# A recurrent scan by halves of the matrix array, more banks for one attention, and a reciprocal root on GpSimd

## Chip, cores and metric

One core of a Trainium2 chip runs the whole program. The metric is device time in microseconds (us) of one execution, lower is better; each kernel is given by the median of several runs. A profile of one execution lies beside the times. Engines are written as in it: PE (TensorE), DVE (VectorE), ACT (ScalarE), POOL (GpSimd), SP (SyncE, which issues most of the loads).

## What is computed

Two transformer blocks in float32, one after the other, on 256 tokens of width 1024. The first block has two layers; layer 0 works on 512 tokens (256 of context, 256 latent), layer 1 puts out the latent ones. Each layer is a mixer and a gated feed-forward net (width 2816), each between a norm with modulation (shift and scale from a conditioning vector) and a norm with a gate. The mixer of layer 0 is what the change is mostly about: a gated delta rule, run over the tokens forwards and backwards in chunks of 64, beside a latent attention (MLA) of 8 heads. Per chunk the rule computes

```
v_new = u_i - w_i @ s                     # s: state, 64x64 per head
o_i   = qd_i @ s + qk_i @ v_new
s     = s * gl_i + kd_i.T @ v_new
```

and the MLA is `softmax(q @ k.T) @ v` with 256 keys for context queries and 512 for latent ones. The second block (sparse attention, a convolution branch, a feed-forward net of 4096) is not touched.

## The kernel before, in words

Every dense weight is loaded from memory as float32, split into a high part (`whi`, rounded by ACT, L270) and a rest (`wlo`, a subtraction, L272), and each product is three matmuls (`mm3`, L552 to L556). `Weights.turn` (L227) says which engine does the subtraction of each next tile: `W.turn("PPPPPP", "V")` gives six tiles to GpSimd and then all to VectorE; `W.turn("V")` gives all to VectorE. A tile has two halves of 128x512, so two subtractions.

PSUM has eight banks of 128x512. In layer 0's mixer they are three of kind "g", two of "s", and one each of "tp", "po" and "gv"; `acc(K)` takes from "s" and `aux(K)` from "g" (L1881). A buffer tagged with `bufs=n` has n copies in turn.

The scan is `gdn_run` (L1216). For each of four rounds and each direction d, `gdn_operands` (L1140) makes u, w, q and decayed k for one tile of 128 tokens (two chunks), in three "g" banks, with 16 + 16 matmuls of 64x64 (L1158, L1160) and four transposes (L1163); ACT copies the results to SBUF (L1165 to L1169), and a matrix Q comes back from memory by a DMA on SP's queue (L1171). Then `gdn_state` (L1183) runs twice, once per chunk: state product w @ s and qd @ s in one bank (L1192), v_new by VectorE (L1195), the update kd.T @ v_new in a second bank (L1199: four matmuls of 64 rows and 128 columns, of whose result two 64x64 blocks on the diagonal are used), state times decay by GpSimd (L1206), the update added by VectorE (L1207), the output product in a third bank (L1210: eight matmuls, all from one half of the rows to the other half of the partitions), and the outputs written or added by `gdn_o` (L1175). A chunk of the tile is addressed as a = 0 or 1, which is the half of the partitions that it lies on; the forward direction takes a = 0, 1, the backward one 1, 0.

After the scan, in program order, come `gdn_post` (norm and gate), six `mod_chunk` calls (L361, matmuls of modulation weights) and `l0_mla` (L787). The MLA has four pairs of heads. For a pair it makes q and k (bank "s" for pairs 0 and 1, "g" for 2 and 3), then per tile of 128 queries `attend` (L665) makes scores in one bank per head, maximum on VectorE, exponential on ACT, transposes on PE (L681) into the same bank, copies to SBUF, and the product with v (L689) in bank "po". `attend` gets two banks' kinds: ("s", "s") for pairs 0 and 1, ("s", "g") for 2 and 3. Its tiles `p` and `pt` have `K.np` = 2 buffers.

Which instruction stands where in an engine's queue is chosen when the kernel is built (`schedule_with_timeline_sim=True`, L2174): program order gives priority, so instructions of the scan, the modulation and the MLA are interleaved on each engine. On the chip each engine then works its queue in order and waits on semaphores.

At the end of layer 0, `linear_deep` (L618) computes the feed-forward net's last product for four tiles of tokens, tile after tile at the end. `post_norm` (L517) consumes it: ACT sums squares, `rstd2` (L340) and `newton` (L310) take the reciprocal root in 8 instructions on one column (L343, L319, three times L322 and L323), VectorE adds the scaled result to h (L542), ACT sums the squares of h (L514), and `norm_tile` (L503) takes a second root, scales the identity by it (L507) and transposes and scales the tile with it on PE (`to_features`, L489), from where ACT and VectorE modulate and split it (L498, L496, L306, L307). Layer 1 then starts with `linear_tok` on its input weights (L1428). Its first six weight tiles are subtracted on GpSimd.

Of the kernel before, what the change touches and what calls it, by code (L numbers as in the profile page):

```python
# [309 lines left out]
def newton(K, v, post=1.0, tag=""):  # L310


    nc = K.nc
    p, n = v.shape[0], v.shape[-1]
    y = sbt(K, [128, 1 if n == 1 else 64], F32, "rsy%d" % (n == 1) + tag, 4)[:, :n][:p]
    t = sbt(K, [128, 1 if n == 1 else 64], F32, "rst%d" % (n == 1) + tag, 2)[:, :n][:p]
    a = -(float(post) / 8192.0) ** (1.0 / 27.0)
    guess = 1597463007.0 + math.log2(-a) * 2 ** 23 - 2.0 ** 31
    nc.vector.tensor_scalar(y.bitcast(I32), v.bitcast(I32), -0.5, float(round(guess)), op0=ALU.mult, op1=ALU.add)  # L319
    for _ in range(3):  # L320
        if n == 1:
            nc.vector.tensor_scalar(t, y, y, v, op0=ALU.mult, op1=ALU.mult)  # L322
            nc.vector.tensor_scalar(y, t, -3.0 * a * a, y, op0=ALU.add, op1=ALU.mult)  # L323
        else:
            nc.vector.tensor_tensor(t, y, y, op=ALU.mult)
            nc.vector.tensor_tensor(t, t, v, op=ALU.mult)
            nc.vector.scalar_tensor_tensor(y, t, -3.0 * a * a, y, op0=ALU.add, op1=ALU.mult)
        a = -2.0 * a ** 3
    return y
# [10 lines left out]
def rstd2(K, ss, tag=""):  # L340

    v = sbt(K, [128, 1], F32, "rsv1" + tag, 2)
    K.nc.vector.tensor_scalar(v, ss[:, 0:1], ss[:, 1:2], D * EPS, op0=ALU.add, op1=ALU.add)  # L343
    return newton(K, v, math.sqrt(D), tag)
# [158 lines left out]
def norm_tile(K, x, ss, coef, hi, lo, t):  # L503


    dg = cut(K, [128, 128], F32, "ndg", 2)
    K.nc.vector.tensor_scalar_mul(dg, K.ident, rstd2(K, ss, "n"))  # L507
    to_features(K, x, coef, hi, lo, t, dg)
# [8 lines left out]
def post_norm(K, G, hdst, after, sq=True, T=2, row=None, held=True):  # L517
# [6 lines left out]
    def consume(c, t, ps):  # L524
# [9 lines left out]
        if c == 1:  # L534
            r = rstd2(K, ss, "p")
# [251 lines left out]
def l0_mla(K, O):  # L787
# [49 lines left out]
    wq = None  # L837
    for pair in range(4):
# [21 lines left out]
        for t in range(4):  # L860
            n = 256 if t < 2 else 512

            def score(pss):
                tk = slice(t * 128, (t + 1) * 128)
                for hh in range(2):
# [4 lines left out]
                   ("s", "g") if late else ("s", "s"))  # L870
        nc.scalar.copy(O[:, pair, :], rb)
        nc.vector.tensor_tensor(O[:, pair, :], po, O[:, pair, :], op=ALU.mult)

# [309 lines left out]
def gdn_state(K, d, first, t, a, u, wq, kd, Q, S):  # L1183
    nc = K.nc
    r = slice(64 * a, 64 * a + 64)
    o = slice(64 - 64 * a, 128 - 64 * a)
# [9 lines left out]
    pS, po = aux(K), aux(K)  # L1196
    for p in range(4):
        c = slice(p * 128, (p + 1) * 128)
        nc.tensor.matmul(pS[:, c], kd[r, c], vn[r, c], start=True, stop=True)  # L1199
    pSv = pS.rearrange("p (q c) -> p q c", q=4)  # L1200
    for hh in range(2):
        x = slice(hh * 64, hh * 64 + 64)
        if first:
            nc.vector.tensor_copy(S[x, :, x], pSv[x, :, x])
        else:
            nc.gpsimd.tensor_tensor(S[x, :, x], S[x, :, x], bc(K.glc[d][x, t, a, :], [64, 4, 64], 2), op=ALU.mult)  # L1206
            nc.vector.tensor_tensor(S[x, :, x], S[x, :, x], pSv[x, :, x], op=ALU.add)  # L1207
    for h in range(8):
        hs = slice(h * 64, h * 64 + 64)
        nc.tensor.matmul(po[o, hs], Q[r, h, :], vn[r, hs], start=True, stop=True)  # L1210
    if not first:
        gdn_o(K, t, a, o, ps)
    gdn_o(K, t, a, o, po)


def gdn_run(K):  # L1216
    K.owritten = set()
    for i in range(4):
        for d in range(2):
            t = i if d == 0 else (1, 0, 3, 2)[i]  # L1220
            ops = gdn_operands(K, d, t)
            for a in ((0, 1) if d == 0 else (1, 0)):
                gdn_state(K, d, i == 0 and a == d, t, a, *ops, K.S[d])
# [651 lines left out]
def layer0(K):  # L1875
# [18 lines left out]
    with Banks(K, {"acc": 5, "aux": 2, "gv": 1}):  # L1894
# [22 lines left out]
        with Pool(K, "ff"):  # L1917
# [8 lines left out]
            with Pool(K, "ffd"):  # L1926
                G = [gate_row(K, 0, s, 1) for s in range(2)]

                def src(g, nk):
# [5 lines left out]
                                      lambda t, ss, x: norm_tile(K, x, ss, coef_mod(K, 1, 0, st(t)), K.uh, K.ul, t), T=4,  # L1935
                                      held=False))
# [31 lines left out]
def layer1(K, h):  # L1968
# [5 lines left out]
    with Pool(K, "l1o"):  # L1974
        load_const(K, "rest", K.cur)
        oh, ol = cut(K, [128, 8, 256], FR), cut(K, [128, 8, 256], FR)
        W.turn("PPPPPP", "V")
# [200 lines left out]
```

## Time and profile before

| | us |
|---|---|
| median of 3 runs | 2125.01 |
| lowest and highest | 2121.82, 2138.47 |
| the profiled execution | 2124.6 |
| its span, first to last instruction | 2122.8 |

Times within the execution are counted from the first instruction. A timeline row gives start and length in us, engine, line of the code, operation, tile written and tiles read (buffer numbers left out), shapes, and the count of instructions merged in the row; in brackets the idle time of the engine before it and what ended it. A float32 matmul of the code shows as two MATMUL records. The granted clock is TensorE's, 1.00 for 2.4 GHz and 0.50 for 1.2 GHz; a value between is a mean over a stretch.

### The profile page before, as it was taken

What the parts mean: (1) busy time and instruction counts of PE and PEld (TensorE: products, weight loads), DVE (VectorE), ACT (ScalarE), POOL (GpSimd) and SP (SyncE); (2) the same over time, 40 slices, a digit from 0 to 9 for tenths busy, and PEclk for the clock granted to TensorE, in tenths of its full rate; (3) what the DMA queues carried; (4) which work ended last, traced back from release to release, by engine and by line L of the source; (5) the groups of instructions that cost most, each with busy time, mean ns of one, the idle gap of its engine ahead of it and who ended that gap; (6) DMA issues with size and microseconds to landing.
All of it is one profiled execution on the core that took longest, in us unless ns stands there. A gap on an engine that the chain in (4) does not pass through costs nothing.

```text
span 2122.8 us, 31144 instructions
## 1 busy us (share of the span) xinstructions
PE 1991.6 (94%) x11656; PEld 1626.7 (77%) x11656; DVE 1315.5 (62%) x2729; ACT 924.7 (44%) x1620; POOL 242.1 (11%) x312
## 2 busy tenths in 40 slices
PE   6989799889999999979898999998999999989998
PEld 3868468768888778868666888897788789868886
DVE  5557457766777754454786555575765558576644
ACT  4533443354222233343565443564554445555532
POOL 2120212301000000020401001110200021020000
PEclk8999789899999999989898999998999999999999
DMA  8344542132568542213235664522656535055551
GB/s 284 90 120 101 179 130 66 46 109 80 179 213 279 164 158 90 89 53 120 70 99 159 184 194 137 155 87 62 197 179 190 180 97 147 21 169 184 188 188 66
DMA packets 186951, 291.88 MB, mean 137 GB/s; under 512 B 28472, under 2 KB 75704, under 8 KB 186800
## 3 DMA queue, kind: packets, MB, share of 16 engines
q1 hardware_dynamic: 172720, 272.54, 41.2%
q0 software_dynamic: 5472, 16.13, 2.4%
q10 hardware_dynamic: 8608, 1.23, 0.5%
q8 instruction: 91, 1.49, 0.3%
q14 instruction: 60, 0.49, 0.1%
HBM read 281.44 MB, written 8.41 MB: 137 GB/s over the span
## 4 chain that ended last, share of the span: by engine, by line
PE 85%; DVE 5%; DMA 4%; ACT 3%; issue 2%; POOL 1%; SPq 0%; ACTq 0%; DVEq 0%; POOLq 0%
PE acc L554 19%; PE acc L556 19%; PE acc L555 19%; PE s L554 3%; PE s L555 2%; PE s L556 2%; PE po L689 2%; PE tp L890 2%; PE po L1540 1%; PE tp L1540 1%; DMA wraw<-in_w_mod_dram 1%; PE gv L373 1%; PE aux L728 1%; PE aux L489 1%; PE g L1199 1%
## 5 line engine op out<-in xcount | busy, mean ns | idle before, releaser
L272 DVE TENSOR_TENSOR wlo<-wraw,whi 128x512 fp32r<-128x512 f32 (+4 forms) x772 | 483.4, 670 | 299.1 <-ACT whi L270 283.3
L270 ACT CAST whi<-wraw 128x1024 fp32r<-128x1024 f32 (+4 forms) x420 | 413.5, 990 | 496.4 <-PE acc L556 192.9
L554 PE MATMUL acc<-whi,u 128*128 128x512 f32 (+3 forms) x1320 | 508.5, 388 | 15.4 <-ACT u L306 9.6
L556 PE MATMUL acc<-whi,u 128*128 128x512 f32 (+3 forms) x1320 | 505.2, 384 | 1.7 <-DVE u L307 1.7
L555 PE MATMUL acc<-wlo,u 128*128 128x512 f32 (+3 forms) x1320 | 506.0, 385 | 0.2 <-DVE wlo L272 0.2
L554 PEld LDWEIGHTS acc<-whi,u 128*128 128x128 f32 x1320 | 251.3, 191 | 66.0 <-ACT u L306 11.6
L556 PEld LDWEIGHTS acc<-whi,u 128*128 128x128 f32 x1320 | 251.0, 190 | 50.4 <-DVE u L307 3.8
L555 PEld LDWEIGHTS acc<-wlo,u 128*128 128x128 f32 x1320 | 251.4, 191 | 47.4 <-DVE wlo L272 1.4
L554 PE MATMUL acc<-u,whi 128*128 128x512 f32 (+1 forms) x480 | 171.0, 362 | 1.8 <-ACT u L306 1.7
L555 PE MATMUL acc<-u,whi 128*128 128x512 f32 (+1 forms) x480 | 171.0, 358 | 0.2 <-DVE u L307 0.2
L556 PE MATMUL acc<-u,wlo 128*128 128x512 f32 (+1 forms) x480 | 171.1, 360 | 0.0
L272 POOL TENSOR_TENSOR wlo<-wraw,whi 128x512 fp32r<-128x512 f32 (+1 forms) x68 | 84.7, 1276 | 409.7 <-ACT whi L270 409.7
L432 DVE SCALAR_TENSOR_TENSOR msum<-mraw,u,msum 128x512 f32<-128x512 f32 x140 | 100.8, 747 | 15.2 <-DMA mraw<-in_w_mod_dram 14.1
L554 PEld LDWEIGHTS acc<-u,whi 128*128 128x128 f32 x480 | 91.0, 191 | 17.4 <-issue 2.6
L555 PEld LDWEIGHTS acc<-u,whi 128*128 128x128 f32 x480 | 91.9, 192 | 15.0 <-issue 1.7
L556 PEld LDWEIGHTS acc<-u,wlo 128*128 128x128 f32 x480 | 91.5, 191 | 15.0 <-issue 1.7
L307 DVE TENSOR_TENSOR u<-aux,u 128x512 fp32r<-128x512 f32 (+2 forms) x96 | 59.5, 632 | 41.0 <-ACT u L306 40.8
L554 PE MATMUL acc<-whi,dxh 128*128 128x512 f32 x176 | 69.7, 396 | 1.9 <-ACT dxh L306 1.9
L306 ACT CAST u<-aux 128x512 fp32r<-128x512 f32 (+2 forms) x96 | 50.6, 543 | 47.6 <-PE aux L728 34.9
L555 PE MATMUL acc<-wlo,dxh 128*128 128x512 f32 x176 | 69.6, 396 | 0.0
L556 PE MATMUL acc<-whi,dxl 128*128 128x512 f32 x176 | 69.0, 396 | 0.0
L307 DVE TENSOR_TENSOR dxl<-u,dxh 128x1024 fp32r<-128x1024 f32 x22 | 26.7, 1225 | 52.5 <-ACT dxh L306 52.5
(521 smaller groups left out, 3089.6 us busy)
## 6 DMA issues: line engine op xcount, KB each, us to landing
wraw<-in_w_up_dram SPq DMA_DIRECT2D x64, 512.0 KB, 4.0
wraw<-in_w_down_dram SPq DMA_DIRECT2D x64, 512.0 KB, 4.0
mraw<-in_w_mod_dram SPq DMA_DIRECT2D x56, 512.0 KB, 4.7
wraw<-in_w_ffn_down_dram SPq DMA_DIRECT2D x44, 512.0 KB, 3.8
wraw<-in_w_mod_dram SPq DMA_DIRECT2D x40, 512.0 KB, 5.9
wraw<-in_w_ffn_gate_dram SPq DMA_DIRECT2D x48, 256.0 KB, 3.1
wraw<-in_w_ffn_up_dram SPq DMA_DIRECT2D x48, 256.0 KB, 3.6
wraw<-in_w_ffn_gate_dram SPq DMA_DIRECT2D x20, 512.0 KB, 4.5
```

The lines of the kernel that those rows point to most:

```text
L270: self.K.nc.scalar.copy(hi, raw)
L272: e.tensor_tensor(lo[:, k], raw[:, k], hi.bitcast(F32)[:, k], op=ALU.subtract)
L306: (hi_eng or nc.scalar.copy)(hi, src)
L307: nc.vector.tensor_tensor(lo, src, hi.bitcast(F32), op=ALU.subtract)
L373: nc.tensor.matmul(ps[32 * j:32 * j + 32, :], K.cl[:, g + k, :], raw[:, k, :], start=(g + k < 4), stop=(g + k >= 4))
L432: nc.vector.scalar_tensor_tensor(accs[s], raw[:, k, :], c, accs[s], op0=ALU.mult, op1=ALU.add)
L554: mm(ps, ah, bh, start=start, stop=False)
L555: mm(ps, ah, bl, start=False, stop=False)
L556: mm(ps, al, bh, start=False, stop=stop)
L689: nc.tensor.matmul(po[hh * 64:hh * 64 + 64, c:c + 128], v(hh, j), pts[hh][0][:, j * 128:(j + 1) * 128], start=(j == 0), stop=(j == nj - 1))
L890: nc.tensor.matmul(tp[:, t * 128:(t + 1) * 128], x[:, t // 2, t % 2 * 128 + j:t % 2 * 128 + j + 128], dg[j], start=(j == 0), stop=(j == 4))
L1540: nc.tensor.matmul(ps[t][:, c * 128:c * 128 + 128], yp[:, c, t * 128 + j:t * 128 + j + 128] if j < 31 else ones, dg, start=(j == 0), stop= ...
```

## The change

Four edits. The scan runs both directions step by step together, and its state update and output product use 64x64 blocks in alternating halves or quarters of the array. The MLA's attention takes its banks in turn from three (pairs 0 and 1) or six (pairs 2 and 3), with three buffers of `p` and `pt`. At the end of layer 0 the reciprocal roots of the post-norm and of the norm after it are on GpSimd. At the start of layer 1 all weight subtractions are on VectorE.

```diff
-def newton(K, v, post=1.0, tag=""):
+def newton(K, v, post=1.0, tag="", eng=None):
+    eng = eng or nc.vector
-    nc.vector.tensor_scalar(y.bitcast(I32), v.bitcast(I32), -0.5, float(round(guess)), op0=ALU.mult, op1=ALU.add)
+    eng.tensor_scalar(y.bitcast(I32), v.bitcast(I32), -0.5, float(round(guess)), op0=ALU.mult, op1=ALU.add)
     for _ in range(3):
         if n == 1:
-            nc.vector.tensor_scalar(t, y, y, v, op0=ALU.mult, op1=ALU.mult)
-            nc.vector.tensor_scalar(y, t, -3.0 * a * a, y, op0=ALU.add, op1=ALU.mult)
+            eng.tensor_scalar(t, y, y, v, op0=ALU.mult, op1=ALU.mult)
+            eng.tensor_scalar(y, t, -3.0 * a * a, y, op0=ALU.add, op1=ALU.mult)
...
-def rstd2(K, ss, tag=""):
+def rstd2(K, ss, tag="", eng=None):
-    K.nc.vector.tensor_scalar(v, ss[:, 0:1], ss[:, 1:2], D * EPS, op0=ALU.add, op1=ALU.add)
-    return newton(K, v, math.sqrt(D), tag)
+    (eng or K.nc.vector).tensor_scalar(v, ss[:, 0:1], ss[:, 1:2], D * EPS, op0=ALU.add, op1=ALU.add)
+    return newton(K, v, math.sqrt(D), tag, eng)
...
@@ l0_mla
+    used = [0]
+    def unit(kinds):
+        used[0] += 2
+        return [kinds[(used[0] + i) % len(kinds)] for i in range(2)]
+    K.np = 3
     for pair in range(4):
...
-                   ("s", "g") if late else ("s", "s"))
+                   unit(("s", "s", "tp", "g", "g", "g") if late else ("s", "s", "tp")))
...
+    K.np = 2
@@ gdn_state (Q is no longer an argument)
         nc.vector.tensor_tensor(vn[r], u[r], ps[r], op=ALU.subtract)
-    pS, po = aux(K), aux(K)
+        gdn_o(K, t, a, slice(64 - 64 * a, 128 - 64 * a), ps)
+    pS = aux(K)[:, :256].rearrange("p (q c) -> p q c", q=4)
     for p in range(4):
-        c = slice(p * 128, (p + 1) * 128)
-        nc.tensor.matmul(pS[:, c], kd[r, c], vn[r, c], start=True, stop=True)
-    pSv = pS.rearrange("p (q c) -> p q c", q=4)
+        for hh in range(2):
+            c = slice(p * 128 + hh * 64, p * 128 + hh * 64 + 64)
+            nc.tensor.matmul(pS[hh * 64:hh * 64 + 64, p, :], kd[r, c], vn[r, c], start=True, stop=True)
...
-            nc.vector.tensor_tensor(S[x, :, x], S[x, :, x], pSv[x, :, x], op=ALU.add)
-    for h in range(8):
-        hs = slice(h * 64, h * 64 + 64)
-        nc.tensor.matmul(po[o, hs], Q[r, h, :], vn[r, hs], start=True, stop=True)
-    if not first:
-        gdn_o(K, t, a, o, ps)
-    gdn_o(K, t, a, o, po)
+            nc.vector.tensor_tensor(S[x, :, x], S[x, :, x], pS[x], op=ALU.add)
+    return vn
@@ gdn_run
-        for d in range(2):
-            t = i if d == 0 else (1, 0, 3, 2)[i]
-            ops = gdn_operands(K, d, t)
-            for a in ((0, 1) if d == 0 else (1, 0)):
-                gdn_state(K, d, i == 0 and a == d, t, a, *ops, K.S[d])
+        ts = [i, (1, 0, 3, 2)[i]]
+        ops = [gdn_operands(K, d, ts[d]) for d in range(2)]
+        for s in range(2):
+            vns = []
+            for d in range(2):
+                u, wq, kd, Q = ops[d]
+                a = s ^ d
+                vns.append((64 * a, Q, gdn_state(K, d, i == 0 and s == 0, ts[d], a, u, wq, kd, K.S[d])))
+            po = aux(K)
+            for h in range(8):
+                hs = slice(h * 64, h * 64 + 64)
+                for a, Q, vn in vns:
+                    K.nc.tensor.matmul(po[64 - a:128 - a, hs], Q[a:a + 64, h, :], vn[a:a + 64, hs], start=True, stop=True)
+            for d in range(2):
+                a = s ^ d
+                gdn_o(K, ts[d], a, slice(64 - 64 * a, 128 - 64 * a), po)
@@ layer0 (norm_tile and post_norm take eng and pass it to rstd2)
-                                      lambda t, ss, x: norm_tile(K, x, ss, coef_mod(K, 1, 0, st(t)), K.uh, K.ul, t), T=4,
-                                      held=False))
+                                      lambda t, ss, x: norm_tile(K, x, ss, coef_mod(K, 1, 0, st(t)), K.uh, K.ul, t, nc.gpsimd), T=4,
+                                      held=False, eng=nc.gpsimd))
@@ layer1
-        W.turn("PPPPPP", "V")
+        W.turn("V")
```

## Rows read from the trace of the kernel before

**Rows 1.** The page: busy tenths of TensorE in 40 slices of the span, the clock granted to it in tenths, and the shares of the chain that ended last by engine.
```profile
PE   6989799889999999979898999998999999989998
...
PEclk8999789899999999989898999998999999999999
...
PE 85%; DVE 5%; DMA 4%; ACT 3%; issue 2%; POOL 1%; SPq 0%; ACTq 0%; DVEq 0%; POOLq 0%
```
**Rows 2.** Windows over the scan and the MLA: stretch and its length in us, then busy us and instructions of PE, of PE's weight loads, of DVE, ACT and POOL, the granted clock, the DMA engines' share and GB/s.
```profile
268.90:290.00 21.10, 19.93 (x216) 15.17 (x210) 11.58 (x31) 8.58 (x17) 2.26 (x3) 0.76 0.42 130
290.00:350.00 60.00, 58.90 (x623) 45.23 (x620) 38.02 (x68) 25.14 (x58) 10.80 (x15) 1.00 0.36 110
350.00:392.00 42.00, 39.71 (x409) 33.13 (x407) 28.48 (x49) 14.94 (x37) 8.01 (x12) 0.92 0.05 14
392.00:410.40 18.40, 15.30 (x159) 13.64 (x157) 12.03 (x29) 2.84 (x7) 5.35 (x9) 0.72 0.12 28
410.40:456.50 46.10, 41.26 (x250) 29.53 (x249) 33.06 (x63) 22.54 (x56) 10.70 (x14) 0.93 0.25 81
268.90:456.50 187.60, 175.11 (x1646) 136.71 (x1640) 123.18 (x238) 74.04 (x174) 37.13 (x52) 0.91 0.24 76
```
**Rows 3.** Timeline of PE, 302 to 350 us: single bursts of the scan's matmuls and of the MLA's product with v (L689), at full clock.
```profile
302.25 0.98 PE L1158 MATMUL g<-u,u 64*64 64x64 f32 x27
...
313.92 1.16 PE L1199 MATMUL g<-gvn,gkd 64*128 64x128 f32 x8
315.00 1.14 PE L1210 MATMUL g<-gvn,gQ 64*64 64x64 f32 x16
316.07 0.44 PE L681 MATMUL s<-const_id,p 128*128 128x128 f32 x2
...
343.10 0.85 PE L1160 MATMUL g<-u,gke 64*64 64x64 f32 x32
...
348.68 1.09 PE L689 MATMUL po<-pt,u 128*64 128x128 f32 x14
```
**Rows 4.** Timeline of PE, 393 to 410 us: the scan's last tile, of the backward direction.
```profile
393.93 0.27 PE L1158 MATMUL g<-u,u 64*64 64x64 f32 x2
...
397.36 1.16 PE L1192 MATMUL g<-u,gwq 128*128 128x128 f32 x8 [0.81 <-ACT gwq L1168]
399.69 1.79 PE L1199 MATMUL g<-gvn,gkd 64*128 64x128 f32 x8 [1.18 <-DVE gvn L1195]
401.41 1.96 PE L1210 MATMUL g<-gvn,gQ 64*64 64x64 f32 x16
...
406.49 2.07 PE L1199 MATMUL g<-gvn,gkd 64*128 64x128 f32 x8 [1.11 <-DVE gvn L1195]
408.49 1.96 PE L1210 MATMUL g<-gvn,gQ 64*64 64x64 f32 x16
```
**Rows 5.** Timelines of DVE and PE: the output of the MLA's second pair (L872), the first matmul of its third (q, in bank "g"), and the longest wait of PE after it.
```profile
392.51 0.68 DVE L872 TENSOR_TENSOR u<-po,u 128x512 f32<-128x512 f32 x1
...
410.38 0.79 PE L554 MATMUL g<-u,whiq 128*128 128x512 f32 x1
...
418.70 0.50 PE L554 MATMUL g<-u,q 128*128 128x256 f32 x2 [1.70 <-ACT q L306]
```
**Rows 6.** The boundary between layers 0 and 1. First the window from the last matmul of layer 0's feed-forward net to the first of layer 1, columns as in rows 2; then PE's timeline with the transposes of the second and third tile and that first matmul; then four windows of DVE from 907 to 931, each with one line's instructions alone, in the order L343, L319, L322, L323 (DVE's busy us and count, clock, DMA share, GB/s); then DVE's adds of the third tile and GpSimd's weight subtractions beside them; then a 32-column instruction on GpSimd, the first instruction of an undisturbed root on DVE and the one that uses its result, and from the groups by form a weight subtraction on DVE (busy us, mean ns, idle us before).
```profile
906.40:926.70 20.30, 8.89 (x49) 8.46 (x48) 17.51 (x54) 12.84 (x32) 8.79 (x7) 0.72 0.36 110
...
911.78 3.58 PE L489 MATMUL aux<-ndg,u 128*128 128x128 f32 x16 [3.43 <-DVE ndg L507]
923.34 3.75 PE L489 MATMUL aux<-ndg,u 128*128 128x128 f32 x16 [7.98 <-DVE rsy1p L323]
926.74 0.77 PE L554 MATMUL acc<-whi,u 128*128 128x512 f32 x1
...
907.00:931.00 24.00, 1.05 (x5) 0.72 0.31 93
907.00:931.00 24.00, 0.75 (x5) 0.72 0.31 93
907.00:931.00 24.00, 3.76 (x15) 0.72 0.31 93
907.00:931.00 24.00, 2.86 (x15) 0.72 0.31 93
...
914.93 1.75 DVE L542 SCALAR_TENSOR_TENSOR u<-y,rsy1p,u 128x512 f32<-128x512 f32 x1
916.59 0.74 DVE L542 SCALAR_TENSOR_TENSOR u<-acc,rsy1p,u 128x512 f32<-128x512 f32 x1
...
910.26 5.86 POOL L272 TENSOR_TENSOR wlo<-wraw,whi 128x512 fp32r<-128x512 f32 x4 [1.43 <-ACT whi L270]
...
256.91 0.45 POOL L813 TENSOR_TENSOR u<-u,ropet 128x32 f32<-128x32 f32 x2
...
6.87 0.21 DVE L343 TENSOR_SCALAR rsv<-ss 128x1 f32<-128x1 f32 x1
...
9.04 0.74 DVE L765 TENSOR_SCALAR u<-u,rsy 128x1024 f32<-128x1024 f32 x1
...
L272 DVE TENSOR_TENSOR wloq<-wraw,whiq 128x512 fp32r<-128x512 f32 x3 | 2.0, 687 | 0.0
```

More of the change, by code (lines that the diff above doesn't have):

```diff
@@ L500, in to_features, with norm_tile @@
         split(K, hi[:, k4:k4 + 4, tk], lo[:, k4:k4 + 4, tk], src)
-def norm_tile(K, x, ss, coef, hi, lo, t):
+def norm_tile(K, x, ss, coef, hi, lo, t, eng=None):
     dg = cut(K, [128, 128], F32, "ndg", 2)
-    K.nc.vector.tensor_scalar_mul(dg, K.ident, rstd2(K, ss, "n"))
+    K.nc.vector.tensor_scalar_mul(dg, K.ident, rstd2(K, ss, "n", eng))
     to_features(K, x, coef, hi, lo, t, dg)
@@ L514, in squares, with post_norm @@
     K.nc.scalar.activation(j, h[:, q * 512:q * 512 + 512], AF.Square, accum_out=ss[:, q:q + 1])
-def post_norm(K, G, hdst, after, sq=True, T=2, row=None, held=True):
+def post_norm(K, G, hdst, after, sq=True, T=2, row=None, held=True, eng=None):
     nc = K.nc
@@ L534, in consume @@
         if c == 1:
-            r = rstd2(K, ss, "p")
+            r = rstd2(K, ss, "p", eng)
             s2 = cut(K, [128, 2], F32, "hss", 4)
@@ L1180, in gdn_o, with gdn_state @@
         K.nc.scalar.copy(K.O[o, t, :], ps[o])
-def gdn_state(K, d, first, t, a, u, wq, kd, Q, S):
+def gdn_state(K, d, first, t, a, u, wq, kd, S):
     nc = K.nc
     r = slice(64 * a, 64 * a + 64)
-    o = slice(64 - 64 * a, 128 - 64 * a)
     if first:
@@ L1203, in gdn_state @@
         if first:
-            nc.vector.tensor_copy(S[x, :, x], pSv[x, :, x])
+            nc.vector.tensor_copy(S[x, :, x], pS[x])
         else:
             nc.gpsimd.tensor_tensor(S[x, :, x], S[x, :, x], bc(K.glc[d][x, t, a, :], [64, 4, 64], 2), op=ALU.mult)
-            nc.vector.tensor_tensor(S[x, :, x], S[x, :, x], pSv[x, :, x], op=ALU.add)
-    for h in range(8):
-        hs = slice(h * 64, h * 64 + 64)
-        nc.tensor.matmul(po[o, hs], Q[r, h, :], vn[r, hs], start=True, stop=True)
-    if not first:
-        gdn_o(K, t, a, o, ps)
-    gdn_o(K, t, a, o, po)
+            nc.vector.tensor_tensor(S[x, :, x], S[x, :, x], pS[x], op=ALU.add)
+    return vn
 def gdn_run(K):
```

## The prediction

> **What bounds the kernel now.** I read the slices and the chain of the page first: TensorE carries 85% of the chain that ends last and most of its slices are full, so an edit pays where it takes matmul time away, or where the PE digit is not 9 [rows 1]. The change touches the sixth to ninth of the 40 slices (9, 9, 8, 8) and the eighteenth (7). I then split the stage of the scan and the MLA attention by windows. From 268.9 to 456.5 us (187.6 us) TensorE is busy 175.1 us at a mean granted clock of 0.91, VectorE 123.2 us, ScalarE 74.0 us [rows 2]. From 290 to 350 TensorE is full at full clock: scan, modulation and attention are interleaved there and the stretch is limited by matmul time. From 392 to 410.4 the scan is alone (attention writes its second pair out at 392.51, and the third pair's first matmul starts at 410.38 [rows 5]): PE is busy 15.3 of 18.4 us at clock 0.72, a mix of 2.4 and 1.2 GHz. So the scan's end releases the third pair: this stretch is latency, not work. From 410.4 to 456.5 two attention pairs run: PE 41.3 of 46.1, clock 0.93. The second place is 906.4 to 926.7: PE does 8.9 us of work in 20.3 us, its transposes of the second and third tile wait 3.43 and 7.98 us, and VectorE is busy 17.5 [rows 6], so VectorE is what the boundary between the layers waits for.
>
> **The scan's matmuls.** Every float32 matmul shows as two records. The state update (L1199) is four 128-column matmuls with 64 rows: eight records, 313.92 to 315.00, 1.08 us. The output product (L1210) is eight 64-column matmuls in one quarter of the array: sixteen records, 315.00 to 316.07, 1.07 us, 67 ns each [rows 3]. The change makes the update eight 64x64 matmuls that alternate between the column halves, and puts the two directions' output products alternately into opposite quarters. Both patterns have a neighbour in the trace. L689 alternates column halves: 14 records of 128 columns in 1.09 us, 78 ns against 135 ns for L1199 (1.08/8), a factor 0.58. L1158 alternates opposite quarters: 27 records in 0.98 us, 36 ns against 67 ns, a factor 0.54, and L1160, over all four quarters, 32 in 0.85 us, 27 ns [rows 3]. So an update costs 16 x 67 x 0.58 = 0.62 us instead of 1.08: 0.46 saved, 16 states, 7.4 us. Two output products cost 32 x 36 = 1.15 us instead of 2.14: 0.99 saved, 8 pairs, 7.9 us. The state products (L1192), the operands, VectorE's subtractions and adds stay in number and size. With the tail of the last record inside those row lengths, the saving is 15 us by the rows and up to 19 if both run in exactly half of 1.08 and 1.07. I take 17, because records in the middle of a row follow each other faster than its length over its count. Below, the bound is 0: nothing overlaps.
>
> The same rows bear on a rule that speaks against this. L1158 writes both row halves into one PSUM bank and still takes 36 ns per record. The Trainium skill (TensorEngine Tiling (Array Packing), Gotcha 1: PSUM Pressure) says that different row tiles cannot access the same PSUM bank simultaneously; the changed output product puts two row halves into one bank too. By that rule the 7.9 us would not be saved; by the row it is. I go by the row.
>
> **The scan's order.** Both directions' operands now come before either's state, and their steps alternate. Before, the last round of the backward direction runs by itself: first operand matmul 393.93, state product 397.36, update 399.69 after waiting 1.18 us for VectorE, output 401.41, second update 406.49 after another 1.11 us, last output until 410.4 [rows 4]. The update takes 1.79 and 2.07 us there instead of 1.16: half clock. Now the forward direction's last round runs inside these waits. At full clock the 15.3 us of work would be 15.3 x 0.72 = 11.0, so 18.4 - 11.0 = 7.4 us is the most to win; I take 4, since VectorE's chain (subtract, then add, for both directions) remains, lower bound 0. Against it: operand buffers come in pairs, and a round now holds both, so the next round's operands and its Q load wait for this round's last product. A set takes 397.36 - 393.93 = 3.4 us from first matmul to first state product [rows 4]; before, it also had to wait for the three "g" banks, so I cost this at 0 and keep 3 later rounds x 3.4 = 10 us as its upper end. The cover is attention's matmuls: gone once pairs 0 and 1 are finished, as after 392.
>
> **MLA banks and buffers.** A third bank and a third p/pt buffer for pairs 0 and 1, six banks for pairs 2 and 3. No instruction is added; scores and transposes of the next tile can be issued while a softmax is on ACT and VectorE. What it can remove is the idle 46.1 - 41.3 = 4.8 us and the clock loss 0.07 x 46.1 = 3.2 us of the last two pairs [rows 2], of which one wait, at 418.70, is 1.70 us for ACT's cast of q and not for a bank [rows 5]. I take 3, from 0 to 8. While the scan runs it lets attention run further ahead, which matters only for who fills the gaps.
>
> **The boundary between layers.** For the four tiles of the last post-norm and the norm after it, the root (8 instructions of one column) goes from VectorE to GpSimd; the first six weight splits of layer 1 go the other way. In 907 to 931 VectorE's share of these small instructions is 1.05 + 0.75 + 3.76 + 2.86 = 8.4 us [rows 6], of which some 6.9 before 926.7 (scaled by 20.3/24 and rounded down). Added before the first layer-1 matmul: three split tiles of two, 6 x 0.687 = 4.1 us [rows 6]; the other tiles fall where VectorE has room. While GpSimd does its four splits at 910.26 to 916.1, VectorE's add takes 1.75 instead of 0.74 us [rows 6]; a second instruction like it and a subtraction lose about as much, so 2.6 us come back. Net on VectorE: -6.9 + 4.1 - 2.6 = -5.4 us. A root on GpSimd: two instructions of 32 columns take 0.45 us there, 0.22 each, so 8 take 1.8 us, perhaps 2.4 with the hops between engines; on VectorE an undisturbed one takes 9.04 - 6.87 = 2.2 us [rows 6]. That is even, and GpSimd has nothing else to do then. Since VectorE is busy 17.5 of the 20.3 us, I take 5 of the 5.4. Bounds: 4 us slower, if GpSimd's roots come one behind another (five in the gap, 0.8 us each too long); 11 faster, if only one tile's chain remains (about 9.5 us: square 0.8, root 2, add 1.5, squares 1, root 2, scaling 0.3, transposes 1.9). What is late next is ACT's casts of the weights and its squares, 12.8 us in the gap.
>
> **Sum.** The profiled execution took 2124.6 us, 1.8 of it outside its span of 2122.8; the median shown, 2125.0, is 0.4 above, so they can be used alike. 17 + 4 + 3 + 5 = 29 us: 2124.6 - 29 = 2095.6, said as 2096. The rest of the program is issued as before.
>
> **Rivals.**
> (a) VectorE becomes the bound of the scan's stage. For: 123.2 us busy there, and its steps stand in every chain; a stage shortened by 24 us has it at 123/164 = 75%, in strict order. Against: from 350 to 392 it is at 28.5/42 = 68% while PE is still at 39.7 [rows 2]. Then a third of the 24 us remains, 8, and with the boundary's 5 the time is 2112. Chance 0.19.
> (b) The two row halves of the output product don't overlap, because they write one bank or because the built order puts other matmuls between them: the change then doesn't do what it says. The 17 shrinks to 9: 2104. For: the trace shows this pattern in the operands' line alone. Against: its 36 ns, with both row halves in one bank [rows 3]. Chance 0.08. This is where the rule of TensorEngine Tiling (Array Packing) in the Trainium skill would leave it.
> (c) Scan and attention overlap so well that no idle PE time is left: 187.6 - 175.1 = 12.5 us of idle and 17 of work go, and the boundary shrinks to one chain (11): 40 us, 2084. For: in 290 to 350 PE is at 58.9 of 60. Against: VectorE's 123 us would be at 78%. Chance 0.17.
> (d) Slower: the clock. Less matmul work with the same waits leaves TensorE more gaps; behind gaps like those of 392 to 410 it was granted 0.72. The remaining 175.1 - 17 = 158 us of PE time at 0.91 become 158 x 0.91/0.72 = 200 us if the whole stage runs at 0.72, with the 12.5 us of idle 212: 25 us longer than now, less 5 at the boundary, 2145. It decides from a stage clock of 158 x 0.91/(187.6 - 12.5 + 5) = 0.80 down. For: 0.76 in the first 21 us. Against: 1.00 and 0.92 over the 102 us between. Chance 0.06.
>
> **How the numbers follow.** The forecast has 0.50. 1% is 21.3 us, about what a measurement of this kernel can tell from no change, so faster means under 2103.8. The forecast's own range is 2086 to 2107 and holds most of its chance below that: 0.43; (c) adds 0.17, half of (b) 0.04 and a little of (a) 0.03: 0.67. Slower is (d), 0.06. The rest, 0.27, lies within 1%. The range takes in (c) with 6 us for the scan's waits, and (a) with 6 us for the operands of later rounds: 2078 to 2118; (d) and the far ends are left out.
>
> **What would show it.** Right: the update's 16 records in 0.5 to 0.65 us and 32 alternating output records in 1.0 to 1.2; the last scan matmul some 20 us or more earlier than 410; MLA's last tile at 430 to 436 instead of 456; PE's idle stretch between the layers near 15 us, with no weight split on GpSimd in it. Wrong: output records at 67 ns; PE idle for VectorE's subtraction in every round; a stage clock under 0.8; the first layer-1 matmul waiting for a root on GpSimd, or for a split on VectorE. The prediction fails if the stage from 268.9 to the last MLA tile shrinks by under 12 us.

## The result and the profile after

The changed kernel took 2094.6 us (median of 4 runs, 2093.0 to 2097.4) beside 2123.9 for the kernel before (4 runs): a ratio of 0.985, 95% interval 0.980 to 0.990. Run once more with the experiments it gave 0.987 (0.985 to 0.989), 28 us less. The forecast was 2096. Its total came out; the sizes of its four terms mostly did not, and the rest of this text is mostly about those.

The page of the changed kernel, rows as in [rows 1]:

```profile
PE   6989799999999999799979998998999999989998
...
PEclk9999799999999999899999999998999999999999
...
PE 82%; DVE 6%; DMA 4%; ACT 3%; issue 2%; POOL 1%; ACTq 0%; SPq 0%; DVEq 0%; POOLq 0%
```

Slices six to nine, where the change lies, have a 9 in both rows now. The same stage by windows, columns as in [rows 2], from the first operand matmul of the scan to the last MLA tile; the scan's last matmuls end at 374.8:

```profile
266.50:290.00 23.50, 20.29 (x381) 15.91 (x379) 15.07 (x35) 12.29 (x27) 4.50 (x6) 1.00 0.49 153
290.00:350.00 60.00, 57.11 (x780) 43.41 (x780) 43.63 (x77) 25.53 (x60) 15.13 (x20) 1.00 0.32 103
350.00:374.80 24.80, 20.61 (x285) 16.76 (x283) 20.52 (x44) 8.76 (x23) 6.33 (x10) 0.93 0.08 24
374.80:422.60 47.80, 45.03 (x330) 33.80 (x329) 41.13 (x79) 27.45 (x69) 11.69 (x16) 1.00 0.24 80
266.50:422.60 156.10, 143.03 (x1769) 109.86 (x1768) 120.34 (x234) 74.03 (x175) 37.65 (x52) 0.99 0.28 91
```

The stage fell from 187.6 to 156.1 us [rows 2]. PE's idle time did not shrink (12.5 and 13.1 us). Busy time by clock, 175.1 x 0.91 = 159.3 and 143.0 x 0.99 = 141.6, gives 17.7 us less PE time at full clock (which is not all due to the matmuls' shapes, as the runs below show); the other 14 us were time at the slow clock (187.6 x 0.09 = 16.9 before, 156.1 x 0.01 = 1.6 now). Not all of that belongs to the change. In the first 23 us the clock was 0.76 before and 1.00 after, but two more kernels with the same scan and attention (two of the experiments below) had 0.84 and 0.83 in that stretch, and one with the old scan had 1.00: up to 5 us of this pair of traces (21.1 x 0.24) may be chance.

PE's timeline, single bursts of the changed scan, with its last round and the third attention pair's first matmul:

```profile
301.07 0.68 PE L1210 MATMUL g<-gvn,gkd 64*64 64x64 f32 x16
301.68 1.16 PE L1201 MATMUL g<-u,gwq 128*128 128x128 f32 x8
...
307.26 1.09 PE L1238 MATMUL g<-gvn,gQ 64*64 64x64 f32 x29
308.29 1.16 PE L1201 MATMUL g<-u,gwq 128*128 128x128 f32 x8
...
368.72 0.68 PE L1210 MATMUL g<-gvn,gkd 64*64 64x64 f32 x16 [1.16 <-DVE gvn L1204]
...
373.77 1.10 PE L1238 MATMUL g<-gvn,gQ 64*64 64x64 f32 x29
...
376.91 0.40 PE L555 MATMUL g<-u,whiq 128*128 128x512 f32 x1
```

An update is 0.61 us (301.07 to 301.68) instead of 1.08, and 29 of the 32 output records of both directions take 1.03 us to the next burst, 36 ns each instead of 67 [rows 3]. The last round runs at full clock; its update took 1.79 and 2.07 us before [rows 4].

At the boundary the gap from the first transposes to layer 1's first matmul grew, from 20.3 [rows 6] to 22.1 us. The window (columns as above), then PE, then DVE, then GpSimd:

```profile
872.81:894.94 22.13, 9.10 (x49) 8.67 (x48) 14.88 (x29) 12.77 (x32) 13.13 (x34) 0.64 0.32 101
```
```profile
872.81 1.95 PE L490 MATMUL aux<-ndg,u 128*128 128x128 f32 x16
881.08 3.75 PE L490 MATMUL aux<-ndg,u 128*128 128x128 f32 x16 [6.32 <-DVE ndg L508]
891.54 3.75 PE L490 MATMUL aux<-ndg,u 128*128 128x128 f32 x16 [6.70 <-DVE ndg L508]
...
902.21 1.95 PE L490 MATMUL aux<-ndg,u 128*128 128x128 f32 x16
```
```profile
877.06 2.50 DVE L272 TENSOR_TENSOR wlo<-wraw,whi 128x512 fp32r<-128x512 f32 x4 [0.30 <-ACT whi L270]
880.65 0.29 DVE L508 TENSOR_SCALAR ndg<-const_id,rsy1n 128x128 f32<-128x128 f32 x1 [1.10 <-POOL rsy1n L324]
...
891.10 0.29 DVE L508 TENSOR_SCALAR ndg<-const_id,rsy1n 128x128 f32<-128x128 f32 x1 [1.87 <-POOL rsy1n L324]
...
896.33 0.69 DVE L307 TENSOR_TENSOR u<-u,u 128x512 fp32r<-128x512 f32 x1
```
```profile
877.15 1.25 POOL L324 TENSOR_SCALAR rsy1n<-rst1n,rsy1n 128x1 f32<-128x1 f32 x1
878.50 1.11 POOL L324 TENSOR_SCALAR rsy1p<-rst1p,rsy1p 128x1 f32<-128x1 f32 x1
...
885.04 0.29 POOL L344 TENSOR_SCALAR rsv1n<-hss 128x1 f32<-128x1 f32 x1 [2.61 <-ACT yj L515]
...
885.94 0.61 POOL L100 DMA_DIRECT2D const_rest<-in_const_rest_dram  x1 [0.33 <-issue]
...
890.80 0.27 POOL L324 TENSOR_SCALAR rsy1n<-rst1n,rsy1n 128x1 f32<-128x1 f32 x1
...
894.94 0.29 POOL L344 TENSOR_SCALAR rsv1n<-hss 128x1 f32<-128x1 f32 x1 [2.60 <-ACT yj L515]
...
896.42 0.81 POOL L323 TENSOR_SCALAR rst1n<-rsy1n,rsv1n 128x1 f32<-128x1 f32 x1
...
898.14 0.27 POOL L324 TENSOR_SCALAR rsy1n<-rst1n,rsy1n 128x1 f32<-128x1 f32 x1
```

VectorE is busy 14.9 us instead of 17.5 and now waits for GpSimd (brackets). A root alone on GpSimd takes from 894.94 to 898.41, 3.5 us, against 2.2 on VectorE [rows 6]; the one of 885.04 ends at 891.07, 6.0 us, because another root is interleaved with it and the issue of a DMA stands between them (0.61 us). And while VectorE subtracts for layer 1 (877.06 to 879.56), single one-column instructions on GpSimd take 1.25 and 1.11 us. In the root alone, one takes 0.81 us beside another 128x512 subtraction on VectorE (896.33), so half a microsecond of its 3.5 comes from there.

Outside these two places nothing moved that can be told from chance: the stretch between them took 449.9 us before and 450.2 after. What lies before the scan (269.0 and 266.5) and behind the boundary (1196.1 and 1198.9) ran from 262.6 to 269.0 and from 1194.6 to 1211.0 over all kernels below, in code that none of them changes. So parts are read from the stage and the gap of the traces, and from medians with their intervals.

### The profile page after: what moved, and what is told of

The parts are those of the page before. It is cut to its first block, busy times and chain, and to the rows that moved or that the text cites. A ratio compares the mean times of both kernels' runs of the same rounds, so it can differ in the third digit from the quotient of the medians.

```text
span 2093.8 us, 31406 instructions
## 1 busy us (share of the span) xinstructions
PE 1958.5 (94%) x11784; PEld 1598.4 (76%) x11784; DVE 1304.3 (62%) x2677; ACT 926.5 (44%) x1622; POOL 246.8 (12%) x364
## 4 chain that ended last, share of the span: by engine, by line
PE 82%; DVE 6%; DMA 4%; ACT 3%; issue 2%; POOL 1%; ACTq 0%; SPq 0%; DVEq 0%; POOLq 0%
PE acc L555 19%; PE acc L557 19%; PE acc L556 19%; PE s L555 3%; PE s L556 2%; PE s L557 2%; PE tp L899 2%; PE po L1558 1%; PE po L690 1%; PE tp L1558 1%; PE gv L374 1%; DMA wraw<-in_w_mod_dram 1%; PE aux L490 1%; PE aux L729 1%; ACT whi L270 1%
## 5 line engine op out<-in xcount | busy, mean ns | idle before, releaser
L272 DVE TENSOR_TENSOR wlo<-wraw,whi 128x512 fp32r<-128x512 f32 (+4 forms) x784 | 489.2, 668 | 300.5 <-ACT whi L270 293.9
L555 PEld LDWEIGHTS acc<-u,whi 128*128 128x128 f32 x480 | 89.7, 188 | 17.2 <-issue 2.6
L272 POOL TENSOR_TENSOR wlo<-wraw,whi 128x512 fp32r<-128x512 f32 (+1 forms) x56 | 67.4, 1235 | 261.5 <-ACT whi L270 261.5
```

The costliest lines, as they stand in the source:

```text
L272: e.tensor_tensor(lo[:, k], raw[:, k], hi.bitcast(F32)[:, k], op=ALU.subtract)
L555: mm(ps, ah, bh, start=start, stop=False)
```

## The experiments

Each time is given as a ratio to the kernel before, run beside it (medians of that kernel in the three groups: 2125.7, 2128.6, 2123.7 us), with its 95% interval, and as microseconds, (ratio - 1) x 2124. The stage is the scan and the attention, scan's first operand matmul to the last MLA tile.

**The scan's edits alone** (against the whole change).
```diff
-                   unit(("s", "s", "tp", "g", "g", "g") if late else ("s", "s", "tp")))
+                   ("s", "g") if late else ("s", "s"))
-        W.turn("V")
+        W.turn("PPPPPP", "V")
```
The third buffers (`K.np`) go too, and the roots are on VectorE.

> Only the scan's edits (order, update in halves, output products alternating); the attention keeps its two banks, the boundary is as before. Theory A: the stage of scan and attention lost 31 us almost wholly to the scan, 17 to 18 of matmul time and some 14 of time at the slow clock, and the attention's extra banks add at most 3: 2094 to 2098 us. Rival B: the extra banks are what fills the scan's waits, so without them the slow-clock time stays: the 14 us come back, 2106 to 2110 us.

Measured: 2105.6 us, 0.9918 (0.9902 to 0.9934), 17 less. Between the two, nearer to B; the stage is 167.5 us at clock 0.98. The slow-clock time went without the banks, against B, yet the stage is 12 us longer than in the whole change, against A's 3. Its window is shown below, with the order with the old shapes.

**The attention's edits alone** (scan and boundary as before; against the kernel before):
```diff
-                   ("s", "g") if late else ("s", "s"))
+                   unit(("s", "s", "tp", "g", "g", "g") if late else ("s", "s", "tp")))
```


> Only the attention's banks in turn and the third buffers of p and pt; scan and boundary as before. Theory A: little, since the two pairs after the scan keep their work and the scan keeps its end: 2119 to 2124 us, 0 to 5 below the kernel before. Rival B: attention runs further ahead and fills the gaps by itself: 2108 to 2114 us.

Measured: 2126.6 us, 1.0019 (1.0003 to 1.0035): 4 us slower. Both theories missed the sign. The stage's windows, first the one where the scan is alone; then the output of attention's second pair, and PE's last rows of the scan:

```profile
378.00:412.40 34.40, 29.81 (x280) 26.55 (x280) 18.03 (x39) 4.82 (x12) 8.29 (x13) 0.60 0.09 23
262.60:454.60 192.00, 178.24 (x1638) 141.97 (x1638) 123.91 (x239) 74.91 (x175) 37.22 (x52) 0.86 0.23 72
```
```profile
376.99 0.69 DVE L880 TENSOR_TENSOR u<-po,u 128x512 f32<-128x512 f32 x1 [0.41 <-PE po L690]
```
```profile
405.35 2.07 PE L1201 MATMUL g<-u,gwq 128*128 128x128 f32 x8
408.53 2.07 PE L1208 MATMUL g<-gvn,gkd 64*128 64x128 f32 x8 [1.10 <-DVE gvn L1204]
410.53 1.96 PE L1219 MATMUL g<-gvn,gQ 64*64 64x64 f32 x16
...
412.43 0.79 PE L555 MATMUL g<-u,whiq 128*128 128x512 f32 x1
```

With more banks attention's second pair is done at 377.7 us, its output 114 after the stage's start instead of 124 (117 in a second trace of the old arrangement), and then has nothing to run: the third pair starts only behind the scan. The scan is alone for 34 us instead of 18, at clock 0.60. The cover was spent early. Two changes to attention are joined here and below, the banks and the third buffers of `p` and `pt`; no run takes the buffers by themselves.

**The boundary's edits alone** (scan and attention as before; against the kernel before):
```diff
-                                      held=False))
+                                      held=False, eng=nc.gpsimd))
...
-        W.turn("PPPPPP", "V")
+        W.turn("V")
```
`norm_tile` is given `nc.gpsimd` in the same call.

> Only the boundary's edits: both roots on GpSimd, all weight subtractions of layer 1 on VectorE. Theory A: the chain of the roots on GpSimd (8 dependent instructions, 3.5 us instead of 2.2) now ends last, and the gap grows by 2: 2124 to 2128 us, 0 to 4 above the kernel before. Rival B: the gap is as the change's trace shows it only because other work moved with it, and VectorE's freed time pays: 2117 to 2121 us.

Measured: 2129.9 us, 1.0017 (0.9999 to 1.0035), 0 to 7 us slower; the gap is 22.0 us. A holds, B falls.

**Everything but the boundary's edits** (the diff above the other way round, against the whole change).

> The whole change without its boundary edits. Theory A: the boundary edits cost 2 us, so this is faster than the whole change: 2091 to 2094 us, the gap between the layers 20 to 21 us. Rival B: the boundary edits are worth 3 to 5 us elsewhere: 2097 to 2100 us.

Measured: 2096.7 us, 0.9876 (0.9851 to 0.9901); the whole change has 0.987 (0.985 to 0.989). The gap is 20.3, as A has it, but the 2 us can't be told in the time, nor can B's 3 to 5 be excluded: the two differ by 1 us with some 7 either way.

**The whole change again.**


> The whole change once more, beside the others of this group. Theory A: 2 us above the version without the boundary edits, 2094 to 2099 us. Rival B: the boundary edits pay, and it is 3 or more below that version: under 2094 us.

Measured: 2101.4 us, 0.987 (0.9847 to 0.9892); stage 154.8, gap 22.0. Against the version without the boundary edits it is 1 us lower by the ratios, which decides for neither theory; the stage and the gap are those of the first trace.

**The order with the old shapes** (attention as changed, boundary as before).
```diff
-    pS = aux(K)[:, :256].rearrange("p (q c) -> p q c", q=4)
+    pS = aux(K)
     for p in range(4):
-        for hh in range(2):
...
+        c = slice(p * 128, (p + 1) * 128)
+        nc.tensor.matmul(pS[:, c], kd[r, c], vn[r, c], start=True, stop=True)
...
-            for h in range(8):
-                for a, Q, vn in vns:
+            for a, Q, vn in vns:
+                for h in range(8):
```


> The scan's new order with the old shapes (update as four matmuls of 128 columns, one direction's output products after the other's); attention's banks as changed, boundary as before. Theory A: the stage is limited by matmul time at full clock, so the 17 us that the halves save come back in full: 2110 to 2116 us. Rival B: the order gives the gain and the saved matmul time would have lain in waits for VectorE: 2098 to 2104 us.

Measured: 2117.2 us, 0.9958 (0.9934 to 0.9982). Against the version with the halves and no boundary edits the halves are worth 17 us in time (0.9958 - 0.9876, on 2124), with 10 to 25 as the interval. A holds in time. The traces give less: this stage is 168.8 us, against 160.9 and 154.8 in two kernels with the halves and the same banks (everything but the boundary's edits, the whole change again), so 8 to 14 us. And this trace is the one with 1211.0 us behind the boundary, where no code differs, so the 17 may hold some chance. The stage's windows, here, in the scan's edits alone and in the whole change again:

```profile
264.60:433.40 168.80, 162.04 (x1640) 127.88 (x1638) 120.86 (x231) 73.47 (x174) 38.72 (x52) 0.95 0.26 82
```
```profile
265.20:432.70 167.50, 150.04 (x1768) 111.91 (x1766) 121.27 (x233) 73.77 (x174) 37.70 (x52) 0.98 0.27 84
```
```profile
264.70:419.50 154.80, 143.24 (x1772) 109.90 (x1766) 119.53 (x233) 73.84 (x175) 37.66 (x52) 0.99 0.29 92
```

**The order alone** (the diff just above and that of the first experiment together).

> The scan's new order alone: old shapes, attention's two banks, boundary as before. Theory A: the scan no longer ends alone at the slow clock, which is worth 10 to 17 us of its own: stage 170 to 177 us, 2107 to 2116 us. Rival B: the order is worth the 4 us of the forecast, and the halves with it make the rest: stage 181 to 185, 2119 to 2122 us.

Measured: 2112.6 us, 0.9951 (0.9933 to 0.9969), 10 us less. A holds, at its lower end in time and past it in the stage (179.0). PE at the scan's end, the output of attention's second pair, and the stage's windows:

```profile
380.75 1.90 PE L1236 MATMUL g<-gvn,gQ 64*64 64x64 f32 x32
382.57 0.50 PE L555 MATMUL g<-u,whiq 128*128 128x512 f32 x1
```
```profile
406.89 0.69 DVE L879 TENSOR_TENSOR u<-po,u 128x512 f32<-128x512 f32 x1
```
```profile
382.40:407.60 25.20, 20.12 (x123) 14.24 (x121) 19.29 (x37) 9.05 (x20) 9.82 (x13) 0.93 0.29 86
407.60:442.30 34.70, 32.07 (x223) 23.07 (x222) 24.67 (x42) 18.65 (x50) 1.59 (x3) 1.00 0.16 46
263.30:442.30 179.00, 164.32 (x1638) 126.55 (x1638) 124.78 (x239) 73.92 (x174) 38.07 (x52) 0.96 0.25 78
```

The third pair starts when the scan ends, as before, but now the second pair still has 24 us to go (its output, 406.9). The tail has changed hands: attention ends last, not the scan.

Without the extra banks the halves are worth 7 us in time (0.9951 - 0.9918, interval 2 to 12) and 11.5 in the stage (179.0 to 167.5); with the banks it was 17 in time and 8 to 14 in the stage. That the banks make the halves worth more is therefore not shown. PE's busy time by clock falls by 11 us with the halves at two banks (164.3 x 0.96 - 150.0 x 0.98) and by 12 with more (162.0 x 0.95 - 143.2 x 0.99). The banks alone, with the same matmuls, take 4 to 6 us off it: 157.7 to 153.9 with the new order, 159.3 to 153.3 (178.2 x 0.86) with the old scan. So of the 17.7 us between the first two traces about 12 belong to the halves and 5 to the banks; why the banks shorten PE's busy time is not known.

**The whole change with two banks for the first two pairs.**
```diff
-                   unit(("s", "s", "tp", "g", "g", "g") if late else ("s", "s", "tp")))
+                   unit(("s", "s", "tp", "g", "g", "g") if late else ("s", "s")))
```


> The whole change, but pairs 0 and 1 of the attention keep their two banks; pairs 2 and 3 have six. Theory A: of the 12 us by which the attention's banks shorten the changed stage, some 4 to 5 belong to pairs 2 and 3 and 7 to 8 to the first two pairs, which run ahead under the scan and so end sooner after it: stage 162 to 165 us instead of 155 to 156, the time 7 above the whole change. Rival B: all of it belongs to pairs 2 and 3: stage 155 to 157, no difference in time.

Measured: 2108.2 us, 0.9923 (0.9901 to 0.9944); stage 165.2. 11 us above the whole change (0.9923 - 0.9870), so A holds, by 0.2 us over its range in the stage. Its split holds too: from the second pair's output to the end it takes 30.9 us here and 35.4 in the scan's edits alone, 4.5 us for the last two pairs. That the whole stage is only 2.3 us shorter than there comes from a second pair that ended 2.2 us later, less than such times vary between traces with the same scan and attention (table below).

**The old scan with more banks for the last two pairs only** (against the kernel before):
```diff
-                   ("s", "g") if late else ("s", "s"))
+                   unit(("s", "s", "tp", "g", "g", "g") if late else ("s", "s")))
```
The third buffers of `p` and `pt` are there for all pairs, in this kernel as in the one above.


> The scan and the boundary as before, pairs 2 and 3 of the attention with six banks, pairs 0 and 1 with two. Theory A: the loss of 4 to 5 us that the banks made beside the old scan comes from pairs 0 and 1, which run ahead and leave the scan's end without cover; without that only the 4 us of pair 3 and a little of pair 2 remain, as a gain: stage 180 to 184 us, 3 to 6 below the kernel before. Rival B: banks taken from the scan cost it the time: the stage stays at 188 to 192.

Measured: 2121.8 us, 0.9988 (0.9967 to 1.0008); the stage 180.6 us at clock 0.92. The stage is as A says; the time, 7 less to 2 more, leaves room for A's smallest gain and for none. B's 188 to 192 is not there: it is the first pairs' banks that hurt the old scan (7 us in time against more banks for all, interval 2 to 12).

These traces together, all in us from the stage's start (scan: start of its last matmul; pair 2: start of its output; pair 3: first matmul; end: last MLA tile). Each row is one trace; rows that differ only in what stands in brackets have the same scan and attention:

| scan, banks | scan | pair 2 | pair 3 | end | clock |
|---|---|---|---|---|---|
| old, two (before) | 141.1 | 123.5 | 141.4 | 187.4 | 0.91 |
| old, two (boundary's edits alone) | 135.4 | 117.3 | 135.6 | 183.1 | 0.94 |
| old, more for all | 149.6 | 114.4 | 149.8 | 192.0 | 0.86 |
| old, more for late | 138.6 | 120.7 | 138.8 | 180.6 | 0.92 |
| new order, two | 119.1 | 143.6 | 119.3 | 179.0 | 0.96 |
| new order, more for all | 120.5 | 137.8 | 123.7 | 168.8 | 0.95 |
| order and halves, two | 107.2 | 132.1 | 108.1 | 167.5 | 0.98 |
| order and halves, more for late | 105.8 | 134.3 | 106.5 | 165.2 | 0.98 |
| order and halves, more for all (again) | 107.1 | 123.8 | 109.3 | 154.8 | 0.99 |
| order and halves, more for all (no boundary edits) | 113.3 | 129.9 | 115.5 | 160.9 | 0.94 |

An end varies by 4 to 6 us between traces of unchanged code (183.1 and 187.4; 154.8 to 160.9 in the six with the changed scan and attention), so a difference of a few microseconds between two rows shows nothing. The lengths from the last release to the end vary much less. With the old scan the end is the third pair's start plus 46 to 47.5 us (42 with more banks): the scan bounds the stage. With the new order it is the second pair's output plus 35.4 (30.9 to 31.0 with more banks, in all traces): attention bounds it. So more banks for the first pairs, with those of the late ones in place, cost 11 us of stage under the old scan (180.6 to 192.0; 7 in time, 1.0019 - 0.9988) and gain 4 to 10 under the new (165.2 to 160.9 and 154.8; 11 in time, 0.9923 - 0.9870, interval 5 to 18).

**Roots on GpSimd, layer 1's subtractions on GpSimd too** (against the whole change, as the next two).
```diff
-        W.turn("V")
+        W.turn("PPPPPP", "V")
```


> The whole change, but with layer 1's first six weight tiles on GpSimd again, so that GpSimd has both the roots and the subtractions. Theory A (GpSimd's chain of roots ends last at the boundary): the subtractions now stand in the same queue as the roots, the gap between the layers grows from 22 to 24 to 28 us, and the time is 2 to 6 us above the whole change. Rival B (it is VectorE's queue that ends last, with the subtractions in it): the gap shrinks to 18 to 20 us, 2 to 4 below the whole change.

Measured: 2100.2 us, 0.9871 (0.9841 to 0.9901); the gap is 24.7 us. A holds and B falls by the gap; in time no difference shows.

**Roots on VectorE, subtractions on VectorE.**
```diff
-                                      held=False, eng=nc.gpsimd))
+                                      held=False))
```
Here `norm_tile` is without `nc.gpsimd` as well.

> The whole change, but with the roots on VectorE again; layer 1's subtractions stay on VectorE. Theory A: 4.1 us of subtractions are added to a VectorE that is busy 17.5 of 20.3 us, and the 2.6 us that GpSimd's subtractions cost it come back: the gap is 20 to 22 us, the time within 2 us of the whole change, and never better than without both edits by more than 1. Rival B: GpSimd's subtractions were the whole slowing, each root in VectorE's queue then takes 2.2 us: the gap is 16 to 18 us, 4 to 6 us below the whole change.

Measured: 2101.1 us, 0.9876 (0.9853 to 0.9899); gap 20.9 us. A holds and B falls by the gap; the times are not told apart.

**One root of two on GpSimd**: the same line of the diff alone; `norm_tile` keeps `nc.gpsimd`.

> The whole change, but only the root of the norm on GpSimd, that of the post-norm on VectorE again; layer 1's subtractions all on VectorE. Theory A (either engine alone is too much for one queue: 22.0 us with both roots on GpSimd, 20.9 with both on VectorE): the two share them and the gap between the layers is 17.5 to 20 us; in time 1 to 4 us below the whole change, which may not show. Rival B: the chain of one tile goes from engine to engine and costs as much: 20.5 to 22 us.

Measured: 2093.3 us, 0.9851 (0.9827 to 0.9875): not told apart from the whole change in time, with the gap that A gives (19.6 us). The gaps of these three, in this order:

```profile
868.51:893.24 24.73, 9.11 (x50) 8.68 (x48) 11.80 (x23) 12.56 (x30) 18.91 (x39) 0.60 0.30 90
```
```profile
870.28:891.22 20.94, 9.05 (x49) 8.68 (x48) 18.85 (x62) 12.71 (x32) 0.53 (x1) 0.72 0.34 107
```
```profile
876.35:895.99 19.64, 8.98 (x50) 8.52 (x48) 16.55 (x43) 12.10 (x30) 7.16 (x17) 0.74 0.39 114
```

Neither VectorE's busy time nor the longer of the two sets the gap: the change has the shortest longer queue of the five (14.9 us on VectorE) and a gap of 22.1. With the roots or the subtractions on GpSimd the gaps go with GpSimd's busy time: 19.6 us (7.2 busy), 20.3 (8.8, before), 22.1 (13.1, the change), 24.7 (18.9). With GpSimd nearly idle (0.5) and all of it on VectorE (18.9 busy) it is 20.9. So the gap is shortest when the roots are shared; what sets it is not shown beyond this. From the first tile's transposes to the fourth's it is 27.4 us here, 29.4 in the whole change, and 29.6 in the kernel before, whose fourth tile is

```profile
936.03 1.95 PE L489 MATMUL aux<-ndg,u 128*128 128x128 f32 x16
```

It is the shortest boundary of all; as a faster kernel it is not shown.

## Why the prediction was right, and where it was not

**The scan's matmuls: rates right, size open.** Foretold: an update of 0.62 us, two output products in 1.15, 17 us in all. Measured: 0.61 us and 36 ns a record (32 x 36 = 1.15). For the size, old and new shapes were set against each other twice under the same order and banks: 7 us (2 to 12) and 17 (10 to 25) in time, 11.5 and 8 to 14 in the stage, 11 and 12 by busy time and clock. That is nearer to the 15 of the rows than to the 17 that I took. The "up to 19" was a wrong sum: half of 1.08 for 16 updates and half of 1.07 for 16 output products is 17.2, so 17 was the upper end and not a middle. The 17.7 us between the first two traces looks like the forecast but holds some 5 us of the banks. Rival (b) falls: the two row halves of the output product write one bank and still overlap. That is also where the rule of the Trainium skill (TensorEngine Tiling (Array Packing), Gotcha 1: PSUM Pressure) does not describe this trace: by it the records would have stayed at 67 ns.

**The scan's order: mechanism right, size wrong.** I took 4 us of at most 7.4, from the 18.4 us in which the scan's last round was alone. By itself the order gave 10 in time (7 to 14; 4 to 8 in the stage, 187.4 and 183.1 to 179.0). The failing step was to count only a shorter wait inside that round. What the runs show is a change of who ends last: with the order alone the scan ends 16 to 22 us earlier in the stage (119.1 against 135.4 and 141.1), the third pair starts then, and it overlaps the second pair's remaining 24 us. No stretch of scan alone is left. The cost that I feared for later rounds' operands is not to be seen in that.

**The attention's banks: wrong as a term.** I priced them at 3 us from the last two pairs, and of running ahead under the scan I wrote that it "matters only for who fills the gaps". That was the point. They cost 4 us with the old scan (1 to 7), and save 9 with the new (0.9918 to 0.9876, interval 3 to 15). The last two pairs, which I priced, bring 4.5 us from the second pair's output to the end (35.4 to 30.9), near the 3; the rest is the first two pairs, which I left at nothing. A single price can't hold for an edit whose sign depends on another edit. In one place the two measures disagree: with the order and the old shapes the banks take 10 us off the stage (179.0 to 168.8) and nothing off the time (0.9951 and 0.9958, 6 either way).

**The boundary: wrong.** I took 5 us of gain; the gap grew by 1.8 and the time of these edits alone is 0 to 7 us slower. The step that failed is the root on GpSimd, 1.8 to 2.4 us from a 32-column instruction of 0.22. A chain of dependent one-column instructions starts one every 0.31 to 0.92 us there, 3.5 us for a root alone and 6.0 when two interleave; the longest of them stand beside VectorE's subtractions. The lower bound that I gave, 4 us slower if GpSimd's roots come one behind another, was near the mechanism: they interleave. VectorE did become freer by 2.6 us, about half of the 5.4 foretold, and spent it waiting. Counted to the fourth tile's transposes the edits are even (29.6 and 29.4).

**The total: right by compensation.** 17 + 4 + 3 + 5 = 29. Step by step in times the runs give: order 10, halves on top 7, banks on top of both 9, the boundary 0 within 7 either way: 26, and 28 for the whole change. Taken so, the order and the banks were 12 too small together, the halves 10 and the boundary 5 too large; in the sequence order, banks, halves it is 10, nothing and 17. That the sum came to 29 is luck as far as its parts go. The first two traces show it as well: the stage shrank by 31 us (22 to 33 over all traces of both) instead of 24, the gap grew by 1.8 instead of shrinking by 5. Of the signs that I named, the two rates and the earlier end of the scan came (374.8 instead of 410); the last MLA tile came earlier (422.6) than the 430 to 436, and the gap of 15 did not come.

**Rivals.** (a) VectorE as the bound: no; it is at 86% from 374.8 to 422.6, but PE is at 94% there; in the scan's last 25 us (350 to 374.8) both are at 83%, and PE waits 1.16 us for VectorE in the last round, so some of that wait is left. (c) no idle PE: PE's idle time is as before, 13 us; the clock gave what the idle time did not. (d) a slower clock: it rose to 0.99. In the one kernel where attention's cover was spent early, the stage fell to 0.86 and the time did rise: the mechanism exists, with 4 us for a price and the old scan for a condition.

**Open.** Whether the version with one root is faster than the change, whether the boundary edits cost or gain a few microseconds in time, and whether the halves are worth more with the banks than without: the intervals are 10 us wide. Why the clock in the stage's first 25 us is 0.75 in some traces and 1.00 in others, and why more banks shorten PE's busy time, is not known.

## What to carry to other kernels

When two chains share an engine, find first which of them ends the stage, and price each edit against the chain that will end it after the other edits: the same extra banks lost 4 us with the old scan and gained 9 with the new. Filler that runs ahead is cover taken from the end of the other chain, as long as that chain ends last. One trace of each kernel is not enough for a difference of a few microseconds: here the same stage took 154.8 to 160.9 us. Before a short dependent chain goes to another engine, take its price from a chain on that engine, not from the length of one wider instruction.

## What the runs showed of the hardware that was not expected

- Subtractions on VectorE slow small instructions on GpSimd as GpSimd's slow VectorE's: while four 128x512 subtractions ran on VectorE, one-column instructions took 1.25 and 1.11 us on GpSimd instead of 0.19 to 0.35. In four traces with this boundary the same six of GpSimd's 64 root instructions take over half a microsecond (0.76 to 1.26), and each overlaps a 128x512 subtraction on VectorE. That GpSimd's lengthen VectorE's was already in [rows 6] (1.75 instead of 0.74).
- 64x64 matmuls that alternate between opposite quarters of the array, with both row halves in one PSUM bank, follow each other at 36 ns a record, 67 ns from one quarter alone; alternating column halves, 16 records in 0.61 us.
- With the old scan alone, PE was busy 29.8 of 34.4 us and its granted clock 0.60, that is four fifths of the stretch at 1.2 GHz, though the engine was 87% busy by the profile.
